# Two feed-forward layers' grouped residual updates moved from VectorE additions to ScalarE copies and accumulating transfers

## The chip, the cores and the metric

The kernel runs on one core of one Trainium2 chip. The metric is the device time of one execution in microseconds (us), the median of a few runs. One execution was also taken by the hardware profiler; its page and its trace are what is read here.

## The reference, cut to what matters

Two layers work on 512 latent tokens and 256 context tokens of width 1024. Each layer is an attention mixer followed by a SwiGLU feed-forward part, and each of the two adds its gated result to the residual stream. The parts that matter here:

```python
def swiglu(h, w_gate_up, w_down):
    g, u = jnp.split(h @ w_gate_up, 2, axis=-1)
    return (jax.nn.silu(g) * u) @ w_down
...
        h_lat = h_lat + g_a * o_lat
        h_lat = h_lat + g_f * swiglu(modulate(h_lat, sh_f, sc_f), ffn_w_gate_up[l], ffn_w_down[l])
        if ctx_out:
            h_ctx = h_ctx + cg_a * o_ctx
            h_ctx = h_ctx + cg_f * swiglu(modulate(h_ctx, csh_f, csc_f), ffn_w_gate_up[l], ffn_w_down[l])
    return rms_norm(h_lat, final_norm)
```

The inner width of the feed-forward part is 2816, that is 22 tiles of 128. `g_f` is one number per feature and stream (latent or context). Context tokens leave the computation after layer 0's feed-forward part, so layer 1 works on the 512 latent tokens alone there.

## The kernel before, in words

Activations are kept transposed: features on the 128 partitions, tokens along the row, so that a residual stream is eight tiles (m = 0 to 7) of 128 features by 768 tokens, of which layer 1 uses 512. Every matrix product is made of three products in a rounded format: each operand is split into a high part (a ScalarE copy that rounds) and a low part (the difference, on VectorE), and TensorE adds high x high, high x low and low x high (lines 319, 321 and 322 in `mm3`; lines 1414 to 1416 in `product`).

The feed-forward part (`ffn`, line 1514) walks through the 22 inner tiles in six groups (`CHUNKS`). For each inner tile, `Pair` loads a gate panel and an up panel (512 KB each, tiles `wr`, three buffers), makes weight combinations and splits on VectorE and ScalarE (`weights`, line 1426), and runs the products. After a group's inner tiles, the *down stage* follows: for each m, `load_w` (line 301) loads the group's part of the down weights (256 KB where the group has four inner tiles, 192 KB where it has three), ScalarE makes the high part (line 308, tiles `wh`, three buffers), VectorE the low part (line 309, tiles `wl`), and TensorE forms the group's contribution to feature tile m in PSUM banks. In layer 0 these are two banks per m (512 latent and 256 context tokens), in layer 1 one bank of 512. For all groups but the last, that contribution goes to the residual's home at once:

- Layer 0 (`down0`, line 1562): the residual lives in DRAM tiles `home`, one per m. GpSimd's queue issues a fetch of `home[m]` into an SBUF tile of the pool `p` (line 1255), VectorE computes bank times gate plus tile (line 1251, twice per m), and GpSimd's queue issues the write back (line 1568).
- Layer 1 (`down1`, line 1672): the residual lives in SBUF tiles `b` (the list `H`). VectorE adds bank times gate to it in place (line 1251, once per m). No transfer is made.

The last group of each layer goes through another function (`final0`, `final1`). `final0` fetches all eight `home` tiles into tiles `b` and adds to those; `final1` works on `H` in halves of 256 tokens and ends in the final norm. Both still use line 1251.

The pool `p` has eight buffers of 128 x 768, shared with two tiles per inner tile (`self.s`, `self.t`) and, in layer 0, with the scratch of `late_mods` (line 257), which computes layer 1's modulation on VectorE (line 273) from weights that GpSimd's queue fetches (line 263). Loads of weights are issued on SyncE's queue (line 134). The order of instructions on every engine is fixed when the program is built: a scheduler works through the code with a simulated timeline and puts each engine's instructions in a row, and every engine takes its row strictly in order, waiting on semaphores where a tile, a bank or a transfer is not ready. `behind` adds orderings for the scheduler.

Of the kernel before, what the change touches and what calls it, by code (L numbers as in the profile page):

```python
# [11 lines left out]
AF = mybir.ActivationFunctionType  # L12
ALU = mybir.AluOpType
# [6 lines left out]
NT = NL + NX  # L20
# [10 lines left out]
LATS = slice(0, NL)  # L31
# [67 lines left out]
def hybrid_kernel(ctx: ExitStack, tc, I, out):  # L99
# [6 lines left out]
    def T(tag, shape, dt=F32):  # L106
        count[0] += 1
        if tag not in SIZES:
            return sb.tile(shape, dt, tag=tag, name=f"{tag}_{count[0]}", bufs=BUFS.get(tag, 1))
        n = int(np.prod(shape[1:]))  # L110
        t = sb.tile([P, SIZES[tag] // (2 if dt == mybir.dt.bfloat16 else 4)], dt, tag=tag, name=f"{tag}_{count[0]}",
                    bufs=BUFS[tag])[: shape[0], :n]
        if len(shape) == 3:
            t = t.rearrange("p (a b) -> p a b", a=shape[1])
        return t

    def B(dt=F32, tag="b"):
        return T(tag, [P, NT], dt)

    def PS(tag):  # L120
        count[0] += 1
        return ps.tile([P, 512], F32, tag=tag, name=f"ps{tag}_{count[0]}", bufs=PBUFS[tag])
# [3 lines left out]
    def PG():  # L126

        ring[0] += 1
        return PS("stsdtsd"[ring[0] % 7])

    V, S, G, PE = nc.vector, nc.scalar, nc.gpsimd, nc.tensor
# [158 lines left out]
    def bg(n=1):  # L290

        for _ in range(n):
            next(mods, None)

    def mod(*which):
        while which not in MOD:
            bg()
        return MOD[which]
# [502 lines left out]
    fetched = []  # L801
# [6 lines left out]
    def chunk(comp, c):  # L808

        o, ins = PM(), []  # L810
        for k in range(KT):
            if k % 2 == 0:
                w = T("st", [P, 512]) if comp == 1 else T(("ph", "pl")[k // 2 % 2], [P, 512])
                fetch(w, I["mod_wp"][PE_MODS.index((0, comp)), c, k // 2])
            g = slice(32 * (k % 4), 32 * (k % 4) + 32)
            ins.append(PE.matmul(o[g, :NX], cond_col[:, k], w[:, NX * (k % 2) : NX * (k % 2) + NX], start=k < 4, stop=k > 3))
        run(ins[0], ins[-1])
        return o
# [54 lines left out]
    for k in range(KT):  # L873
        i = int(k > 5)
# [4 lines left out]
    scale = chunk(1, 0)  # L879
# [357 lines left out]
    H = []  # L1237
    for k in range(KT):
        t = B()
# [4 lines left out]
    def add_residual(m, o, l, comp, v, c, dst=None, base=None):  # L1244
        base = base or H[m]
        if c is TOK2:
            for x, v in pieces(c):
                ins = add_residual(m, o[:, x.start - HT : x.stop - HT], l, comp, v, x, dst, base)
            return ins
        g = mod(l, comp, v, m)  # L1250
        return V.scalar_tensor_tensor((dst or base)[:, c], o, g, base[:, c], op0=ALU.mult, op1=ALU.add)

    def fetched(m, c, tag="p"):
        t = B(tag=tag)
        G.dma_start(t[:, c], home[m][:, c])
        return t
# [61 lines left out]
    home = [dr.tile([P, NT], F32, name=f"home{k}") for k in range(KT)]  # L1318
# [241 lines left out]
    norm1, A = modulated(new, 1, 0, G, LATS)  # L1560

    def down0(m, w, hs):
        t = fetched(m, slice(0, NT))
        o = banks((LATS, CTXS), PG)
        mm3(o, w(), hs)
        for i, (x, c) in enumerate(o):
            ins = add_residual(m, x, 0, 5, i, c, None, t)
        G.dma_start(home[m], t)
        return ins

    def final0(src, hs):
# [5 lines left out]
    H = new  # L1577
# [3 lines left out]
    for k in range(KT):  # L1581
        t = dr.tile([P, NL], F32, name=f"parked{k}")
# [35 lines left out]
    for t0, n in ((0, 4), (4, 2)):  # L1618
        o = PS("t")
# [40 lines left out]
    H = []  # L1660
    for k in range(KT):
        t = B()
# [7 lines left out]
    fn = const("final_norm", [P, 8])  # L1670

    def down1(m, w, hs):
        o = PG()
        mm3([(o, LATS)], w(), hs)
        add_residual(m, o, 1, 5, 0, LATS)

    def final1(src, hs):

# [166 lines left out]
```

## Time and profile before

| what | value |
|---|---|
| times of three runs | 1554.84, 1552.52, 1556.6 us; median 1554.84 |
| profiled execution, first to last instruction (its span) | 1553.0 us, 1.84 us below the median of the three runs and inside their spread |
| busy: TensorE (PE), VectorE (DVE), ScalarE (ACT), GpSimd (POOL) | 98%, 76%, 49%, 13% of the span |
| mean granted TensorE clock | 0.996 |
| moved by transfers | 225.69 MB, mean 145 GB/s |
| feed-forward part of layer 0, of layer 1 | about 450 to 970 us, about 1180 to 1553 us |

How to read it: times inside the trace are microseconds from the span's start. A row of a group of instructions gives line, engine, operation, what it writes and reads, count, total busy time and mean duration in nanoseconds (ns), then the engine's idle time just before and what ended it. "PEld" is the load of weights into TensorE, which overlaps the products. Tiles are named by their pool (`p`, `b`, `wr`, `wh`, `wl`), PSUM banks by `pss`, `pst`, `psd`. Since a product's end is modelled, the time that TensorE loses is read from its waits rather than from its busy share.

### The profile page before, as it was taken

To read this page: it belongs to the slowest core of one execution; us is meant where nothing else is said; L and a number is where in the kernel's file an instruction comes from. 1 tells how busy PE (TensorE), PEld (TensorE's weight loads), DVE (VectorE), ACT (ScalarE), POOL (GpSimd) and SP (SyncE) were. 2 spreads that over 40 slices of the span, in tenths; PEclk is the share of its full clock that TensorE was granted. 3 is DMA by queue.
4 is the path that set the end of the run, shared out by engine and by line. 5 is a ranking of instruction groups with operands and counts; after the bars stand their busy time and mean duration, and the time that the engine had idled before them with its cause. 6 is when DMAs were issued, how large, how long until landed. Compare 5 with 4: busy or idle time off the path is not lost.

```text
span 1553.0 us, 26645 instructions
## 1 busy us (share of the span) xinstructions
PE 1527.4 (98%) x10048; PEld 1375.5 (89%) x10048; DVE 1179.9 (76%) x2418; ACT 758.2 (49%) x1521; POOL 195.1 (13%) x266
## 2 busy tenths in 40 slices
PE   9999999999999999999999999999999999999997
PEld 8788887878999898999989998877789899899997
DVE  4799877776867686777768667789977779678685
ACT  4532676674555242432424335567856445354453
POOL 0022211000111102012021122560011000000001
PEclk9999999999999999999999999999999999999999
DMA  9775654244643636547475493210214223324322
GB/s 320 251 226 176 165 129 106 57 131 136 217 138 119 232 104 216 173 133 287 128 261 175 156 355 137 59 37 1 96 58 161 70 84 127 115 75 136 89 91 87
DMA packets 80930, 225.69 MB, mean 145 GB/s; under 512 B 11232, under 2 KB 18400, under 8 KB 80800
## 3 DMA queue, kind: packets, MB, share of 16 engines
q1 hardware_dynamic: 61968, 148.47, 30.1%
q0 software_dynamic: 17680, 73.94, 13.9%
q8 instruction: 79, 1.29, 0.3%
q10 hardware_dynamic: 1152, 1.57, 0.3%
q14 instruction: 51, 0.42, 0.1%
HBM read 186.97 MB, written 23.07 MB: 135 GB/s over the span
## 4 chain that ended last, share of the span: by engine, by line
PE 85%; DVE 7%; DMA 3%; ACT 2%; issue 2%; POOL 0%; SPq 0%; DVEq 0%; ACTq 0%; POOLq 0%
PE pso L530 5%; PE pss L1416 5%; PE pss L1415 5%; PE pss L1414 5%; PE psd L319 4%; PE pss L319 4%; PE psd L321 4%; PE psd L322 4%; PE pss L322 4%; PE pss L321 4%; PE pst L1416 3%; PE pst L319 3%; PE pst L321 3%; PE pst L1414 3%; PE pst L322 3%; PE pst L1415 3%
## 5 line engine op out<-in xcount | busy, mean ns | idle before, releaser
L308 ACT CAST wh<-wr 128x1024 fp32r<-128x1024 f32 (+2 forms) x148 | 115.6, 795 | 225.1 <-DMA wr<-in_w_dn_dram 39.4
L309 DVE TENSOR_TENSOR wl<-wr,wh 128x1024 fp32r<-128x1024 f32 (+2 forms) x145 | 131.1, 911 | 82.3 <-ACT wh L308 78.1
L537 ACT ACTIVATE p<-p,sm 128x512 f32<-128x512 f32 (+3 forms) x144 | 105.0, 730 | 30.6 <-DVE sm L541 30.1
L1414 PE MATMUL pss<-b,wh 128*128 128x384 f32 (+1 forms) x346 | 107.6, 312 | 0.5 <-ACT b L345 0.5
L1415 PE MATMUL pss<-b,wh 128*128 128x384 f32 (+1 forms) x346 | 107.8, 312 | 0.0
L1416 PE MATMUL pss<-b,wl 128*128 128x384 f32 (+1 forms) x346 | 107.1, 311 | 0.0
L321 PE MATMUL psd<-b,wh 128*128 128x512 f32 (+2 forms) x254 | 88.7, 349 | 0.0
L273 DVE CUSTOM_DVE_ANT_0 p<-rope,cond 128x1024 bf16<-128x1024 f32 x64 | 76.9, 1221 | 12.4 <-DMA rope<-in_mod_w_dram 12.1
L319 PE MATMUL psd<-b,wh 128*128 128x512 f32 (+2 forms) x214 | 79.0, 369 | 0.7 <-ACT wh L308 0.3
L322 PE MATMUL psd<-b,wl 128*128 128x512 f32 (+2 forms) x214 | 77.8, 363 | 0.0
L263 POOL DMA_DIRECT2D rope<-in_mod_w_dram x48 | 25.6, 533 | 412.4 <-DVE mod L273 389.8
L530 PE MATMUL pso<-ph,b 128*64 128x256 f32 (+1 forms) x384 | 77.0, 359 | 0.2 <-DVE ph L475 0.2
L530 PE MATMUL pso<-pl,b 128*64 128x256 f32 (+1 forms) x384 | 76.9, 358 | 0.0
L1416 PE MATMUL pst<-b,wl 128*128 128x384 f32 (+1 forms) x226 | 70.8, 313 | 2.0 <-DVE wl L1402 2.0
L1414 PE MATMUL pst<-b,wh 128*128 128x384 f32 (+1 forms) x226 | 70.7, 313 | 0.6 <-ACT p L1464 0.6
L1401 ACT CAST wh<-pl 128x512 fp32r<-128x512 f32 x78 | 44.9, 619 | 53.0 <-PE pss L1415 22.7
L1415 PE MATMUL pst<-b,wh 128*128 128x384 f32 (+1 forms) x226 | 70.5, 312 | 0.0
L1401 ACT CAST wh<-wr 128x1024 fp32r<-128x1024 f32 x39 | 41.0, 1051 | 57.3 <-PE pst L1415 14.8
L321 PE MATMUL pss<-b,wh 128*128 128x256 f32 (+3 forms) x216 | 68.3, 316 | 0.0
L319 PE MATMUL pss<-st,wh 128*128 128x512 f32 (+2 forms) x198 | 67.5, 341 | 0.3 <-ACT wh L308 0.3
L322 PE MATMUL pss<-st,wl 128*128 128x512 f32 (+2 forms) x198 | 67.6, 341 | 0.1
L1414 PEld LDWEIGHTS pss<-b,wh 128*128 128x128 f32 x346 | 65.0, 188 | 1.0 <-ACT b L345 0.8
(609 smaller groups left out, 5269.4 us busy)
## 6 DMA issues: line engine op xcount, KB each, us to landing
wr<-in_w_gu_dram SPq DMA_DIRECT2D x88, 512.0 KB, 4.0
rope<-in_mod_w_dram POOLq DMA_DIRECT2D x48, 512.0 KB, 3.9
wr<-in_w_dn_dram SPq DMA_DIRECT2D x73, 256.0 KB, 3.0
wr<-in_w_out_dram SPq DMA_DIRECT2D x32, 512.0 KB, 3.8
p<-home POOLq DMA_DIRECT2D x40, 384.0 KB, 5.7
home<-p POOLq DMA_DIRECT2D x40, 384.0 KB, 5.6
wr<-in_w_in_dram SPq DMA_DIRECT2D x21, 512.0 KB, 3.9
ph<-in_mod_w_dram SPq DMA_DIRECT2D x24, 256.0 KB, 3.0
```

What stands on the lines that cost most here:

```text
L273: behind(V.tensor_tensor_reduce(out=T("p", [P, D], mybir.dt.bfloat16), in0=w, in1=cond[:, v, :], op0=ALU.mult, op1=ALU.add, scale=1.0, sca ...
L308: behind(S.copy(h, r), *after[:1])
L309: behind((G if eng else V).tensor_tensor(lo, r, f(h), op=ALU.subtract), *after[1:])
L319: ins = PE.matmul(o, wh[:, k], mh[:, c], start=first and k == 0, stop=False)
L321: PE.matmul(o, wh[:, k], ml[:, c], start=False, stop=False)
L322: PE.matmul(o, wl[:, k], mh[:, c], start=False, stop=last and k == n - 1)
L530: ins = PE.matmul(o[64 * i : 64 * i + 64, c], v(kt), t, start=n == 0, stop=n == len(moving[i]) - 1)
L537: S.activation(p[:, c], p[:, c], AF.Exp, bias=nm, scale=-1.0, accum_out=dn)
L1401: S.copy(h, t)
L1414: PE.matmul(o, wh, xh, start=first and k == 0, stop=False, skip_group_check=not first)
L1415: PE.matmul(o, wh, xl, start=False, stop=False, skip_group_check=not first)
L1416: PE.matmul(o, wl, xh, start=False, stop=k == 3, skip_group_check=not first)
```

## The change

Inside the groups, VectorE no longer makes the residual update. ScalarE copies the bank times the gate into a tile of the pool `p` (an ACTIVATE with Copy and a per-partition scale), and GpSimd's queue issues a transfer that adds this tile to the residual's home: in layer 0 to the DRAM tile `home[m]`, in layer 1 to the SBUF tile `H[m]`. Layer 0's fetch within groups disappears. The last group of each layer is as before.

```diff
+    def gated(dst, o, g):
+        return S.activation(dst, o, AF.Copy, scale=g)
+
...
     def down0(m, w, hs):
-        t = fetched(m, slice(0, NT))
+        t = B(tag="p")
         o = banks((LATS, CTXS), PG)
         mm3(o, w(), hs)
         for i, (x, c) in enumerate(o):
-            ins = add_residual(m, x, 0, 5, i, c, None, t)
-        G.dma_start(home[m], t)
+            ins = gated(t[:, c], x, mod(0, 5, i, m))
+        G.dma_start(home[m], t, accum_op=ALU.add)
         return ins
...
     def down1(m, w, hs):
-        o = PG()
+        o, t = PG(), B(tag="p")
         mm3([(o, LATS)], w(), hs)
-        add_residual(m, o, 1, 5, 0, LATS)
+        gated(t[:, LATS], o, mod(1, 5, 0, m))
+        G.dma_start(H[m][:, LATS], t[:, LATS], accum_op=ALU.add)
```

The new code is three lines longer above the feed-forward part, so the lines there are numbered higher by three (1401, 1402, 1436 become 1404, 1405, 1439); the copy is line 1254, the fetch of line 1255 becomes line 1258, the accumulating transfers are lines 1571 and 1679. The scheduler places the other instructions anew around it. TensorE has as many rows as before; where the order differs, a few products that used to stand early as fillers stand later.

On ScalarE, at the end of layer 1's first group, the high parts of the down weights (line 308) stood in one run before the next pair's weights (line 1401, tile `wr` to `wh`, `ph`):

```order
L308 CAST wh_13301<-wr_13299 128x384
L308 CAST wh_13318<-wr_13316 128x384
L308 CAST wh_13335<-wr_13333 128x384
L308 CAST wh_13352<-wr_13350 128x384
L308 CAST wh_13369<-wr_13367 128x384
L1401 CAST wh_13389<-wr_13385 128x1024
L1401 CAST ph_13413<-wr_13386 128x512
L1401 CAST wh_13391<-ph_13398 128x512
```

The same place now:

```order
L308 CAST wh_13325<-wr_13323 128x384
L1254 ACTIVATE p_13265<-pst_13264,mod_1831_8978 128x512
L308 CAST wh_13344<-wr_13342 128x384
L1254 ACTIVATE p_13284<-pss_13283,mod_1831_8978 128x512
L1404 CAST wh_13365<-wr_13361 128x1024
L1254 ACTIVATE p_13303<-psd_13302,mod_1831_8978 128x512
L1254 ACTIVATE p_13322<-pss_13321,mod_1831_8978 128x512
L1404 CAST ph_13389<-wr_13362 128x512
L1404 CAST wh_13367<-ph_13374 128x512
```

Each copy of a bank stands in ScalarE's row between the casts of weights, and the last ones stand among the casts of the next pair's weights.

On VectorE, at the same boundary, the preparation of the next pair (lines 1402 to 1444) stood among the last residual updates:

```order
L309 TENSOR_TENSOR wl_13370<-wr_13367,wh_13369 128x384
L1251 SCALAR_TENSOR_TENSOR b_12135<-psd_13332,mod_1831_9010,b_12135 128x512
L1402 TENSOR_TENSOR wl_13390<-wr_13385,wh_13389 128x1024
L1436 TENSOR_TENSOR pl_13397<-wr_13386 128x512
L1251 SCALAR_TENSOR_TENSOR b_12137<-pss_13349,mod_1831_9010,b_12137 128x512
L1437 TENSOR_TENSOR ph_13398<-pl_13397,wr_13385 128x512
L1440 TENSOR_TENSOR ph_13403<-wr_13385,wr_13386 128x512
L1251 SCALAR_TENSOR_TENSOR b_12139<-pst_13366,mod_1831_9010,b_12139 128x512
L1444 TENSOR_TENSOR pl_13409<-wr_13385,ph_13398 128x512
```

The same place now:

```order
L309 TENSOR_TENSOR wl_13345<-wr_13342,wh_13344 128x384
L1405 TENSOR_TENSOR wl_13366<-wr_13361,wh_13365 128x1024
L1439 TENSOR_TENSOR pl_13373<-wr_13362 128x512
L1440 TENSOR_TENSOR ph_13374<-pl_13373,wr_13361 128x512
L1443 TENSOR_TENSOR ph_13379<-wr_13361,wr_13362 128x512
L1447 TENSOR_TENSOR pl_13385<-wr_13361,ph_13374 128x512
```

The updates are gone from VectorE's row, and the preparation of the next pair follows the low parts directly.

On GpSimd's queue, at the end of layer 0's fifth group, writes back and fetches stood mixed; the fetches into `b` are those of `final0`:

```order
L1255 DMA b_9853<-home_4268 128x768
L1568 DMA home_4270<-p_9433 128x768
L1255 DMA p_9510<-home_4272 128x768
L1568 DMA home_4271<-p_9470 128x768
L1255 DMA b_9855<-home_4269 128x768
L1255 DMA b_9857<-home_4270 128x768
L1568 DMA home_4272<-p_9510 128x768
L1255 DMA b_9859<-home_4271 128x768
L1255 DMA b_9861<-home_4272 128x768
```

The same place now:

```order
L1571 DMA home_4271<-p_9432 128x768
L1258 DMA b_9807<-home_4265 128x768
L1258 DMA b_9809<-home_4266 128x768
L1258 DMA b_9811<-home_4267 128x768
L1258 DMA b_9813<-home_4268 128x768
L1571 DMA home_4272<-p_9471 128x768
L1258 DMA b_9815<-home_4269 128x768
L1258 DMA b_9817<-home_4270 128x768
L1258 DMA b_9819<-home_4271 128x768
L1258 DMA b_9821<-home_4272 128x768
```

The last accumulating transfer (into `home_4272`) is still followed by `final0`'s fetch of the same tile. In layer 1 the queue's row now holds forty accumulating transfers and nothing between them.

## The prediction

> **What bounds the kernel now.** I read the page's busy times first, then TensorE's waits in the two feed-forward stretches, then the busy times by stage. The page (busy us, share of the span, instructions):
>
> ```profile
> PE 1527.4 (98%) x10048; PEld 1375.5 (89%) x10048; DVE 1179.9 (76%) x2418; ACT 758.2 (49%) x1521; POOL 195.1 (13%) x266
> ```
>
> TensorE is the bound: it idles for 1553.0 - 1527.4 = 25.6 us in the whole span. VectorE, which the change relieves, is busy for 76%, so its work counts only where TensorE waits for it. The waits of TensorE between 480 and 935 us (layer 0's groups) and between 1230 and 1530 us (layer 1's), each with its sum, number and longest:
>
> ```profile
> PE pst L1416 <- DVE wl L1402: 2.0, 2, 1.4
> PE psd L319 <- DVE p L1251: 0.7, 1, 0.7
> ...
> PE pss L1416 <- DVE wl L1402: 0.6, 2, 0.3
> PE pst L319 <- ACT st L1401: 0.6, 1, 0.6
> ```
>
> These four rows are all there is: 2.7 us in layer 0 and 1.2 us in layer 1, 3.9 us or 0.25% of the time. No relief of an engine other than TensorE can bring more in these stretches. So the question is what of these 3.9 us goes, and what new waits the copies and transfers make.
>
> Busy times by stage: a down stage of layer 0 with the next pair's preparation, layer 1's first boundary, its third, and the pairs behind that. The columns are PE, PEld, DVE, ACT, POOL, the granted clock, the share of the transfer engines and GB/s:
>
> ```profile
> 595.00:640.00 45.00, 44.22 (x251) 39.58 (x250) 29.80 (x52) 11.36 (x19) 10.16 (x19) 1.00 0.72 252
> 1230.00:1250.00 20.00, 19.72 (x106) 16.53 (x105) 17.47 (x30) 8.20 (x16) 0.00 (x0) 1.00 0.46 136
> 1340.00:1358.00 18.00, 18.00 (x93) 15.10 (x92) 14.65 (x23) 7.27 (x13) 0.00 (x0) 1.00 0.55 164
> 1358.00:1402.00 44.00, 44.00 (x343) 42.54 (x343) 32.57 (x55) 22.45 (x45) 0.00 (x0) 1.00 0.24 78
> ```
>
> TensorE is full in all of them. VectorE is the second fullest at layer 1's boundaries (17.47 of 20 us), ScalarE has more than half its time free, and the transfer engines are already much in use in layer 0.
>
> **The change part by part.** *VectorE's updates go.* Their prices, by form:
>
> ```profile
> L1251 DVE SCALAR_TENSOR_TENSOR p<-psd,mod,p 128x512 f32<-128x512 f32 x15 | 11.2, 749 | 3.9 <-PE psd L322 3.5 <-DMA p<-home 0.4
> L1251 DVE SCALAR_TENSOR_TENSOR p<-pss,mod,p 128x256 f32<-128x256 f32 x15 | 7.2, 477 | 0.7 <-PE pss L322 0.7
> L1251 DVE SCALAR_TENSOR_TENSOR b<-pss,mod,b 128x512 f32<-128x512 f32 x19 | 14.2, 747 | 5.5 <-PE pss L322 5.5
> ```
>
> Layer 0 loses 40 x (0.749 + 0.477) = 49 us of VectorE, layer 1 40 x 0.747 = 30 us. All of it lies beside TensorE, except where a wait above hangs on it. Layer 0's longest of those, VectorE's rows and then TensorE's:
>
> ```profile
> 627.74 0.74 DVE L1251 SCALAR_TENSOR_TENSOR p<-pst,mod,p 128x512 f32<-128x512 f32 x1
> 629.60 0.48 DVE L1251 SCALAR_TENSOR_TENSOR p<-pss,mod,p 128x256 f32<-128x256 f32 x1
> 636.58 0.69 DVE L1436 TENSOR_TENSOR pl<-wr 128x512 f32<-128x512 f32 x1 [3.05 <-DMA wr<-in_w_gu_dram]
> ...
> 642.54 0.44 PE L1416 MATMUL pst<-b,wl 128*128 128x384 f32 x1 [1.35 <-DVE wl L1402]
> ```
>
> The two updates stand before the step that frees the buffer for the panel landing at 636.58. Without them the panel is asked for up to 0.74 + 0.48 = 1.2 us earlier; I credit 1.0 of this 1.4 us wait, and the same cause's other wait whole (2.0 - 1.4 = 0.6). The 0.7 us on line 1251 goes with the fetch it depended on. Layer 0 gains 2.3 us.
>
> *ScalarE's copies come.* No row before has a copy from a bank with a per-partition scale. The nearest rows are a copy from a bank with a fixed scale (lines 449 and 1095) and an ACTIVATE with a per-partition operand out of SBUF (line 407):
>
> ```profile
> L449 ACT ACTIVATE b<-psd 128x512 f32<-128x512 f32 x10 | 5.9, 590 | 8.7 <-PE psd L322 8.6
> L1095 ACT ACTIVATE b<-psd 128x256 fp32r<-128x256 f32 x8 | 3.0, 377 | 2.3 <-PE psd L322 2.3
> L407 ACT ACTIVATE b<-p,mod 128x512 fp32r<-128x512 f32 x16 | 11.6, 724 | 10.4 <-DVE mod L828 5.9 <-DVE p L406 4.5
> L407 ACT ACTIVATE b<-p,mod 128x256 fp32r<-128x256 f32 x16 | 7.9, 507 | 10.3 <-DVE p L406 10.3
> ```
>
> So 590 to 724 ns for 512 tokens, 377 to 507 for 256; I take 0.70 and 0.48, nearer to line 407, whose operands it has. Layer 0 adds 40 x 1.18 = 47 us, layer 1 40 x 0.70 = 28 us. At layer 1's third boundary ScalarE goes from 7.27 to 7.27 + 8 x 0.70 = 12.9 of 18 us: not full. The Trainium skill (ScalarE: Activation LUTs, Rules for kernel authors) speaks against the move: multiplications belong on VectorE, up to about three times faster there in bf16. The trace differs for this form, 590 to 724 ns against 747 for the update; by the rule, an estimate of 3 x 747 ns would make 8 copies last 17.9 us, and ScalarE would then be the bound of the down stages.
>
> A copy waits for its bank, and behind it in ScalarE's row stand casts of the next weights, for which VectorE's low parts and then TensorE wait. Before, the update stood in front of the low part in the same way, for 0.75 us; the copy puts 0.70 us in front of the cast instead. I count nothing, with bounds from -0.05 to +0.70 us at each of ten boundaries, most of it covered by ScalarE's idle time.
>
> *Layer 0's transfers.* The page's rows, with KB of one and median us to landing:
>
> ```profile
> p<-home POOLq DMA_DIRECT2D x40, 384.0 KB, 5.7
> home<-p POOLq DMA_DIRECT2D x40, 384.0 KB, 5.6
> ```
>
> Forty fetches go, and forty writes become accumulating ones. No row shows one. It costs at least one copy, and at most, by these rows, the fetch and the write it stands for, 5.7 + 5.6 = 11.3 us until landed. Layer 0's load on the transfer engines therefore falls or stays. The last one meets `final0`'s fetch; the rows of GpSimd's queue and of VectorE's last use:
>
> ```profile
> 923.95 0.54 POOL L1568 DMA_DIRECT2D home<-p  x1
> ...
> 930.46 0.54 POOL L1255 DMA_DIRECT2D b<-home  x1 [5.44 <-issue]
> ...
> 953.84 0.74 DVE L1251 SCALAR_TENSOR_TENSOR b<-pst,mod,b 128x512 f32<-128x512 f32 x1
> ```
>
> A landing of 11.3 us puts the fetch at about 935 us; with 5.7 us more its tile is there at 941, 13 us before its use. No cost.
>
> *Layer 1's transfers are new*: forty of 256 KB. GpSimd has nothing else to do there:
>
> ```profile
> POOL p L1711 <- ACT p L1707: 336.4, 1, 336.4
> ```
>
> But the transfer engines load weights there. A boundary adds 8 x 256 KB = 2.1 MB in 18 us, or 117 GB/s. By the first stage row (0.72 at 252 GB/s) that is a share of 0.33 at the price of one copy and 0.67 at two, on top of 0.55: 0.88 or 1.22. How long panel loads take in such a crowd is seen in layer 0 (612 to 632 us), and in layer 1 without it (1230 to 1300 us):
>
> ```profile
> L134 SPq DMA_DIRECT2D wr<-in_w_gu_dram x5: 327/328/1243, 614.6 to 631.3; - x5
> DMA to landing us min/median/max: 4.4/6.5/10.0
> ...
> L134 SPq DMA_DIRECT2D wr<-in_w_gu_dram x11: 327/328/328, 1236.9 to 1295.3; - x11
> DMA to landing us min/median/max: 3.5/4.1/4.6
> ```
>
> At one copy I expect layer 0's median: panels land 6.5 - 4.1 = 2.4 us later. What VectorE does between the second panel and TensorE's wait at the first boundary:
>
> ```profile
> 1243.28 0.69 DVE L1436 TENSOR_TENSOR pl<-wr 128x512 f32<-128x512 f32 x1
> 1243.88 0.75 DVE L1251 SCALAR_TENSOR_TENSOR b<-pss,mod,b 128x512 f32<-128x512 f32 x1
> ...
> 1245.74 0.74 DVE L1251 SCALAR_TENSOR_TENSOR b<-pst,mod,b 128x512 f32<-128x512 f32 x1
> ...
> 1247.60 0.69 DVE L1402 TENSOR_TENSOR wl<-ph,wh 128x512 fp32r<-128x512 f32 x1
> ...
> 1248.34 0.38 PE L1416 MATMUL pss<-st,wl 128*128 128x256 f32 x1 [0.28 <-DVE wl L1402]
> ```
>
> Two updates leave this chain, about 1.3 us (each is followed 0.66 us later by the next instruction). So 2.4 us late costs 1.1 us at this boundary and at the second, which waits as well (two waits in the row above). The other three show no wait, and I count none: their groups have four inner tiles, not three, so their loads are spread over a longer stage. Layer 1 loses 2.2 us.
>
> Sum: -2.3 + 2.2 = -0.1 us. On the profiled span that is 1552.9 us; on the median, which lies 1.84 us higher, **1554.7 us**.
>
> **The rivals.** *A, slower: the accumulating transfers crowd out layer 1's weight loads.* At two copies the share asked for is 1.22, more than there is, and panels land like layer 0's worst (10.0 us, 5.9 late), or midway (8.25 us, 4.15 late). At the first two boundaries lateness less 1.3 us becomes waiting; at the other three I count half of that. Midway: (4.15 - 1.3) x (2 + 1.5) = 10.0 us, less layer 0's 2.3: 1562.5 us. At the worst, 4.6 x 3.5 - 2.3 = +13.8: 1568.6 us. It decides, by more than 0.3%, from about 3.3 us of lateness (3.5 x 2.0 - 2.3 = 4.7). For it: layer 0's landings. Against it: the 44 us behind each boundary at a share of 0.24 can take what is late, and VectorE's relief of 8 x 0.66 us a boundary may buy more than 1.3. The Trainium skill (DMA: Bandwidth & Descriptors, Issuing engines are not separate DMA queues) states that transfers started from any queue run on the same 16 engines and interleave; by that, GpSimd's queue gives no protection, and layer 0's landings agree with it (4.4 to 10.0 us against 3.5 to 4.6).
>
> *B, slower: long landings hold the pool `p`.* The first update of layer 1's first group and the next pair's first write into `p`:
>
> ```profile
> 1233.44 0.75 DVE L1251 SCALAR_TENSOR_TENSOR b<-pst,mod,b 128x512 f32<-128x512 f32 x1 [0.49 <-PE pst L322]
> ...
> 1246.90 0.36 ACT L1454 COPY p<-pss 128x256 f32<-128x256 f32 x1
> ```
>
> Eight copies take all eight buffers, so that write now needs an early transfer landed within about 13.5 us. Beyond it, each us costs 1 us at five boundaries: a landing of 18.5 us gives +25, 1580 us. Above the 11.3 us bound; nothing in the trace asks for it.
>
> *C, faster: all 3.9 us go and nothing is added*: 1550.9 us. That is 0.25%; it needs run-to-run scatter as well to pass for faster.
>
> **How the numbers follow.** 0.3% is 4.7 us, about what a measurement of this kernel can tell from no change. The forecast (both sides' small waits, within 4.7 us) gets 0.60, A 0.26, B 0.07, and a result faster by more than 0.3% 0.07, C with scatter. So faster 0.07, same 0.60, slower 0.33. The range goes from C less half a us, 1550.4, to A's worst, 1568: below lie some 0.06, above some 0.10. The forecast's own range is 1550.4 to 1559.5.
>
> **What would show it.** Right: TensorE's waits still sum to a few us in both stretches, the wait on line 1251 is gone, the copy takes 0.6 to 0.72 us, panels in layer 1's boundaries land in 5 to 7.5 us, and the accumulating transfers in under 11.3 us. Panels at 4 us with waits gone speak for C; panels over 7.4 us with waits of TensorE on line 1402's low parts or ScalarE's casts on panels for A; line 1457's copies waiting for an accumulating transfer for B. The prediction is wrong if the change lands outside 1550.4 to 1568 us, or if its waits come from another place, such as ScalarE's casts behind a copy.

## The result, and the profile after

The changed kernel takes 1594.05 us (median of 4 runs, 1592.39 to 1599.06), the kernel before 1555.72 us beside it (4 runs). The ratio is 1.0259, with a 95% interval of 1.0242 to 1.0275: 38 us slower, far outside the range that was forecast. The profiled execution has a span of 1590.5 us, 37.5 us more than before.

The page's busy times (busy us, share of the span, instructions):

```profile
PE 1541.7 (97%) x10048; PEld 1385.0 (87%) x10048; DVE 1113.1 (70%) x2298; ACT 818.3 (51%) x1641; POOL 222.0 (14%) x266
```

VectorE's busy time fell by 67 us and ScalarE's rose by 60 us (the prediction had 79 and 75, adding up durations that overlap in the trace), and the time did not fall with it: TensorE now idles for 1590.5 - 1541.7 = 48.8 us, where it idled for 25.6. It is also busy for 14.3 us longer with the same number of products; part of that is its clock (last section). TensorE's waits in the changed kernel, in layer 0 (480 to 960 us) and in layer 1 (1240 to 1545 us), each with sum, number and longest, the smallest rows left out:

```profile
PE pss L1417 <- ACT p L1457: 9.5, 5, 5.2
PE pst L1419 <- DVE wl L1405: 1.1, 1, 1.1
PE pst L1417 <- ACT p L1467: 0.6, 1, 0.6
...
```

```profile
PE pss L1417 <- ACT wh L1404: 7.3, 6, 1.5
PE pst L1417 <- ACT wh L1404: 2.8, 2, 1.5
PE pss L1419 <- DVE wl L1405: 1.9, 5, 0.5
PE psd L1417 <- ACT wh L1404: 1.6, 1, 1.6
PE pst L1419 <- DVE wl L1405: 1.0, 1, 1.0
...
```

In place of the 2.7 and 1.2 us of before stand 12 us in layer 0 and 16 us in layer 1 (the smallest rows included). Most are waits for ScalarE's casts (line 1404) and copies of banks (1457) and for VectorE's low parts (1405), of the pairs that follow a boundary between groups. Both engines are late and not busy. This is the stage around layer 1's third boundary in the changed kernel, with the columns of the prediction's stages:

```profile
1362.00:1388.00 26.00, 22.78 (x125) 19.74 (x124) 14.84 (x23) 13.18 (x24) 6.12 (x8) 0.95 0.94 238
```

Over the five boundaries VectorE is busy for 54 to 57% of such a stage and ScalarE for 46 to 56%. What is full are the transfer engines, at a share of 0.78 to 0.94, where it was 0.45 to 0.52 before. What VectorE and ScalarE are late for is seen in the landings of the panels, in layer 1 (before, then after):

```profile
L134 SPq DMA_DIRECT2D wr<-in_w_gu_dram x38: 327/328/328, 1236.9 to 1493.4; - x38
...
DMA to landing us min/median/max: 3.4/3.7/5.7
```

```profile
L134 SPq DMA_DIRECT2D wr<-in_w_gu_dram x38: 327/328/881, 1249.5 to 1532.0; - x38
...
  DVE pl L1439: 21.4, 9
  ACT ph L1404: 12.8, 8
  ACT wh L1404: 12.5, 5
...
DMA to landing us min/median/max: 3.4/6.0/8.8
```

The same 38 loads land 2.3 us later at the median, and VectorE and ScalarE now wait 47 us for them, where they waited for 8. In layer 0 the median went from 5.3 to 7.4 us. The new transfers are the reason to look at first (the page's issues, KB of one, median us to landing):

```profile
home<-p POOLq DMA_DIRECT2D x40, 384.0 KB, 8.4
...
b<-p POOLq DMA_DIRECT2D x40, 256.0 KB, 6.7
```

To tell the two layers apart I measure two stretches in each trace, because what lies ahead of them varies by some us from one profile to the next. Layer 0 is from the first product of its first pair to the first transfer that parks the residual: 485.4 us before, 498.5 after, **+13.1 us**. Layer 1 is from the first product of its first pair to the start of TensorE's last instruction: 301.4 us before, 325.0 after, **+23.6 us**. The stretch between them is 0.5 us shorter, what precedes them 1.2 us longer: together the 37.4 us of the span. (The first two inner tiles of layer 0 and the first three of layer 1 are made outside `Pair`. The first pair meant here is the first that `Pair` makes, so that layer 1's stretch begins inside its first boundary.) In four of the kernels below layer 0 is left as before, and its stretch came out 1.0 to 1.5 us shorter there; so nothing under 2 us is read from one stretch.

Followed product by product (the starts of the rows of line 1414, now 1417, in their order), the delay grows at the boundaries alone: by about 2.8, 3.3, 5.6, 6.5 and 5.6 us at the five of layer 1, and by 1.2, -0.9, 3.6, 2.2 and 7.0 us at the five of layer 0.

### The profile page after: what moved, and what is told of

It is laid out like the page before. It is cut to its first block, busy times and chain, and to the rows that moved or that the text cites. A ratio compares the mean times of both kernels' runs of the same rounds, so it can differ in the third digit from the quotient of the medians.

```text
span 1590.5 us, 26703 instructions
## 1 busy us (share of the span) xinstructions
PE 1541.7 (97%) x10048; PEld 1385.0 (87%) x10048; DVE 1113.1 (70%) x2298; ACT 818.3 (51%) x1641; POOL 222.0 (14%) x266
## 4 chain that ended last, share of the span: by engine, by line
PE 76%; DMA 9%; DVE 8%; ACT 4%; issue 3%; POOL 0%; DVEq 0%; ACTq 0%; POOLq 0%
DMA wr<-in_w_gu_dram 8%; PE pso L530 5%; PE pss L1419 4%; PE pss L1417 4%; PE pss L1418 4%; PE psd L319 3%; PE pss L319 3%; PE psd L321 3%; PE psd L322 3%; PE pss L321 3%; PE pss L322 3%; PE pst L1419 3%; PE pst L1417 3%; PE pst L1418 3%; PE pst L484 3%
## 5 line engine op out<-in xcount | busy, mean ns | idle before, releaser
L1417 PE MATMUL pss<-b,wh 128*128 128x384 f32 (+1 forms) x346 | 109.7, 317 | 3.8 <-ACT wh L1404 3.3
L1418 PE MATMUL pss<-b,wh 128*128 128x384 f32 (+1 forms) x346 | 109.4, 316 | 0.1
L1679 POOL DMA_DIRECT2D b<-p x40 | 34.6, 878 | 274.5 <-ACT p L1254 222.3
L1439 DVE TENSOR_TENSOR pl<-wr 128x512 f32<-128x512 f32 x39 | 26.9, 689 | 62.6 <-DMA wr<-in_w_gu_dram 62.6
L1419 PEld LDWEIGHTS pss<-b,wl 128*128 128x128 f32 x346 | 66.4, 192 | 3.2 <-DVE wl L1405 3.1
```

Source lines behind the costliest of these rows:

```text
L1417: PE.matmul(o, wh, xh, start=first and k == 0, stop=False, skip_group_check=not first)
L1418: PE.matmul(o, wh, xl, start=False, stop=False, skip_group_check=not first)
L1419: PE.matmul(o, wl, xh, start=False, stop=k == 3, skip_group_check=not first)
```

## The experiments

Three causes were held against each other. *Transfers*: the accumulating transfers fill the transfer engines where the panels of the next pairs are loaded, as rival A said. *ScalarE's time*: the copies hold back the casts. *Turned rows*: without VectorE's updates the scheduler wrote the preparation of the pairs in another order. This is the second pair behind the third boundary of layer 1, VectorE's row before and after (1402 and 1405 with a row of 1024 make the gate panel's low part; the other lines combine gate and up panel):

```
before                                   after
L1436 pl<-wr            (up)             L1439 pl<-wr            (up)
L1455 p<-pss,p                           L1440 ph<-pl,wr
L1402 wl<-wr,wh 1024    (gate, low)      L1443 ph<-wr,wr
L1437 ph<-pl,wr                          L1458 p<-pss,p
L1440 ph<-wr,wr                          L1447 pl<-wr,ph
L1444 pl<-wr,ph                          L1405 pl<-wr,ph         (up, low)
L1402 pl<-wr,ph         (up, low)        L1405 wl<-wr,wh 1024    (gate, low)
```

The gate panel's low part has gone from third place to last, behind everything that needs the up panel, which lands later. On ScalarE the up panel's cast (line 1404, `ph`) now stands ahead of the gate panel's (`wh`). The casts are turned so in three of layer 1's 19 pairs, the second behind the third, the fourth and the fifth boundary. The result is a wait of TensorE for a cast whose panel had long landed. The changed kernel there, two rows of ScalarE and then one of TensorE:

```profile
1380.25 0.62 ACT L1404 CAST ph<-wr 128x512 fp32r<-128x512 f32 x1 [2.71 <-DMA wr<-in_w_gu_dram]
1380.77 1.04 ACT L1404 CAST wh<-wr 128x1024 fp32r<-128x1024 f32 x1
...
1381.86 0.39 PE L1417 MATMUL pss<-b,wh 128*128 128x256 f32 x1 [1.38 <-ACT wh L1404]
```

ScalarE stood idle for 2.71 us until the up panel landed, cast that, and only then cast the gate panel, for which TensorE stood.

The results in one table: median us, ratio to the kernel before with its 95% interval, and the two stretches against before.

| kernel | us | ratio | layer 0 | layer 1 |
|---|---|---|---|---|
| the change | 1594.05 | 1.0259 [1.0242, 1.0275] | +13.1 | +23.6 |
| tiny | 1561.04 | 1.0039 [1.0024, 1.0055] | -3.9 | +10.0 |
| plain | 1565.86 | 1.0076 [1.0044, 1.0109] | -3.3 | +16.4 |
| xfer | 1575.90 | 1.0130 [1.0097, 1.0163] | -1.4 | +19.0 |
| gfirst | 1599.24 | 1.0272 [1.0236, 1.0307] | +11.9 | +21.9 |
| rtiny | 1560.82 | 1.0030 [1.0016, 1.0044] | -3.8 | +7.9 |
| rafter | 1593.95 | 1.0249 [1.0217, 1.0282] | +13.2 | +21.8 |
| rpool | 1581.86 | 1.0168 [1.0146, 1.0189] | -1.0 | +28.1 |
| late | 1579.33 | 1.0153 [1.0134, 1.0172] | -1.5 | +23.4 |
| rtiny2 | 1552.95 | 0.9976 [0.9958, 0.9995] | -4.0 | +1.6 |
| rafter2 | 1588.13 | 1.0182 [1.0146, 1.0219] | +15.7 | +13.7 |
| late2 | 1555.70 | 0.9992 [0.9970, 1.0014] | -1.4 | +0.4 |
| rall | 1572.50 | 1.0101 [1.0078, 1.0125] | +12.9 | +2.5 |
| twice | 1576.74 | 1.0144 [1.0124, 1.0164] | +10.1 | +9.5 |

### tiny: the copies without the transfers

```diff
-        G.dma_start(home[m], t, accum_op=ALU.add)
+        G.dma_start(home[m][:, :8], t[:, :8], accum_op=ALU.add)
-        G.dma_start(H[m][:, LATS], t[:, LATS], accum_op=ALU.add)
+        G.dma_start(H[m][:, :8], t[:, :8], accum_op=ALU.add)
```

> Copies as in the change, but each accumulating transfer moves only 8 of its 768 or 512 columns, in both layers; the rest of the addition is left out. The scheduler then puts the up panel's cast ahead of the gate panel's on ScalarE in six of layer 1's pairs, where the change has it in three and the kernel before in none. Theory T (transfers: the accumulating transfers fill the transfer engines, the next panels land late, TensorE waits): 1549 to 1557 us, panels in layer 1 land in about 3.7 us again. Rival R (ScalarE's row: the copies and the turned order of the casts hold back the high parts): 1580 to 1605 us, with TensorE's waits on ScalarE's casts of layer 1 at 11.7 us or more.

1561.04 us: between the two theories. Layer 0 is 3.9 us shorter than before, so there all of the loss, and more, hangs on the transfers. Layer 1 still loses 10.0 us, although its panels land in 4.2 us at the median. Its waits (1225 to 1510 us) are for low parts on VectorE, the engine that was relieved:

```profile
PE pss L1419 <- DVE wl L1405: 4.3, 5, 1.8
PE psd L1419 <- DVE wl L1405: 1.9, 1, 1.9
```

### plain: the same bytes, the same rows, no addition

```diff
-        G.dma_start(home[m], t, accum_op=ALU.add)
+        G.dma_start(home[m], t)
-        G.dma_start(H[m][:, LATS], t[:, LATS], accum_op=ALU.add)
+        G.dma_start(H[m][:, LATS], t[:, LATS])
```

> The change with plain writes in place of the accumulating transfers, so the old residual is overwritten instead of added to; same bytes, same order of every engine row for row. T, with the price of an accumulating transfer at about two copies: one copy is left, layer 1 loses 8 to 14 us instead of 24 and layer 0 0 to 5 instead of 12, in all 1563 to 1574 us. T, if only the bytes count: 1590 to 1596 us. R: the rows are the same, so 1588 to 1596 us.

1565.86 us, in the range for an accumulating transfer that costs two copies, but by luck: layer 1 lost more than the 8 to 14 us expected, 16.4, and layer 0 gained 3.3 us where none was expected. The price is seen directly in the transfer engines' time (queue, packets, MB, share of the 16 engines), layer 1 after (1240 to 1530 us) and with plain writes (1225 to 1505 us):

```profile
q0 software_dynamic: 5760, 10.49, 21.2%
```

```profile
q0 software_dynamic: 3200, 10.49, 9.3%
```

For the same 40 transfers that is 0.212 x 290 = 61.5 us against 0.093 x 280 = 26.0 us of all engines, or 1.54 against 0.65 us for one: 2.4 copies, in 144 packets in place of 80. With the rows unchanged, 7.2 us of layer 1's loss (23.6 - 16.4) come with the addition. The other 16.4 us split only roughly, into 10.0 us for rows (from tiny, whose rows are not quite the change's) and 6.4 us for plain bytes. Layer 0 gains 3.3 us with plain writes, so its 13.1 us come with the accumulating form; rall and twice ask why.

### xfer: the transfers without the copies

```diff
         add_residual(m, o, 1, 5, 0, LATS)
+        G.dma_start(spare[m], H[m][:, LATS], accum_op=ALU.add)
```

(`spare` stands for eight regions in two tiles that are no longer read.)

> The kernel before, with VectorE's updates in both layers, and in layer 1 one more accumulating transfer of 256 KB per feature tile, from the updated residual to tiles that nobody reads. The gate panel's cast stays ahead of the up panel's in all of layer 1. T: layer 1 loses 15 to 30 us, 1570 to 1585 us in all. R: 1554 to 1558 us, since ScalarE's row is that of before.

1575.90 us, layer 1 +19.0, with VectorE's updates and the gate panel first. Its panels landed in 5.6 us at the median (at most 8.6). So the transfers are enough by themselves: about 2.5 to 5.1 us at each of the five boundaries.

### gfirst, rtiny, rafter: part of the old order

```diff
-            parts(g, *w1, self.after)
+            gate = S.copy(w1[0], g)
+            low = behind(V.tensor_tensor(w1[1], g, f(w1[0]), op=ALU.subtract), *self.after)
...
-            V.tensor_tensor(s4, g[:, h[1]], s2, op=ALU.subtract)
+            behind(V.tensor_tensor(s4, g[:, h[1]], s2, op=ALU.subtract), *(low,) * self.l)
-            self.u2 = parts(u[:, h[1]], T("ph", [P, 512], F32R), T("pl", [P, 512], F32R))
+            up = T("ph", [P, 512], F32R), T("pl", [P, 512], F32R)
+            behind(S.copy(up[0], u[:, h[1]]), *(gate,) * self.l)
+            marks["low"] = V.tensor_tensor(up[1], u[:, h[1]], f(up[0]), op=ALU.subtract)
+            self.u2 = up
```

gfirst has only the ordering of the two casts, on the change; rtiny has both orderings on tiny, rafter both on the change.

> The change with one more ordering, in layer 1 only: the up panel's cast stands behind the gate panel's of the same pair, as it does before. T: the three waits of 1.6 us behind it go in part, 1582 to 1592 us. R: layer 1's loss of 24 us shrinks to under 12, 1570 to 1582 us.

> As the run with 8 columns per transfer (1558.5 us in its profile, of which layer 1's feed-forward part lost 10.0 us against the kernel before), and in layer 1 two orderings more: the gate panel's cast stands ahead of the up panel's on ScalarE, and the gate panel's low part ahead of the last combination (pl from ph) on VectorE. If the turned rows made the 10 us (theory R2): layer 1 loses under 3 us, 1549 to 1553 us in all, since layer 0 gained 3.9. If it is ScalarE's time for the copies (R1): layer 1 still loses 8 us or more, 1556 to 1562 us.

> The change with the same two orderings in layer 1, its full transfers kept. T (transfers) with R2 added to it: layer 1 loses 14 to 19 us instead of 23.6, 1583 to 1590 us in all. T alone, the rows only showing what the late panels leave: 22 us or more, 1590 us or more. R2 alone: under 5 us, 1572 to 1577 us.

gfirst, at 1599.24 us, missed both of its ranges; the scheduler had then put the gate panel's low part behind the last combination in 7 of the 19 pairs in place of 4. The 1.7 us that it won in layer 1 are less than a stretch can tell, and its profile is of an execution 8.4 us below its median. rtiny won 2.1 of 10.0 us and rafter 1.8, which is, within 0.2 us, what was expected if the turned rows cost nothing. By these numbers ScalarE's time for the copies was left. But the rows of rtiny said otherwise: the low part stood fourth of five, ahead of the last combination as asked, where before it stood second. The edit had not restored what it was to test.

### rtiny2, rafter2: the old order, pair by pair

```diff
+            at = 0 if not self.l else 1 if self.j < 9 else 2 if self.j % 2 else 4
+            behind(V.tensor_tensor(s1, u[:, h[0]], u[:, h[1]], op=ALU.add), *self.after, *(low,) * (at == 1))
+            behind(V.tensor_tensor(s2, s1, g[:, h[0]], op=ALU.subtract), *(low,) * (at == 2))
+            behind(V.tensor_tensor(s4, g[:, h[1]], s2, op=ALU.subtract), *(low,) * (at == 4))
```

(These lines replace those that make `s1`, `s2` and `s4`; the cast's ordering is kept.)

> As the run with 8 columns per transfer, and in layer 1 the preparation of each pair is put back into the order that VectorE and ScalarE have in the kernel before: the gate panel's cast ahead of the up panel's, and the gate panel's low part ahead of the first, second or fourth combination, as it stands there pair by pair. The first two orderings alone had left 7.9 of 10.0 us of layer 1's loss. R2 (the turned rows): layer 1 loses under 3 us, 1549 to 1553 us in all. R1 (ScalarE's time for the copies): still 6 us or more, 1555 to 1562 us.

> The change, full transfers, with the same order of the kernel before in layer 1's pairs. If transfers and rows each cost their own: layer 1 loses 12 to 17 us in place of 23.6, 1581 to 1588 us in all. If late panels are enough by themselves, as in the run with transfers alone (19.0 us): 18 to 24 us, 1588 to 1595 us.

With the low part where it stood before in each pair, layer 1 of rtiny2 loses 1.6 us instead of 10.0, and the whole takes 1552.95 us. Its waits in the stretch (1230 to 1510 us) are the few of before:

```profile
PE pst L319 <- ACT st L1404: 0.6, 1, 0.6
PE psd L1419 <- DVE wl L1437: 0.5, 1, 0.5
PE pss L1417 <- ACT p L1462: 0.3, 1, 0.3
```

So the turned rows are shown, and ScalarE's time for the copies costs nothing that can be read. rafter2 takes the same order with the full transfers: +13.7 instead of +23.6. The rows are worth 8.4 us without the transfers and 9.9 with them, so the two causes add up. What rafter2 wins lies at the third to fifth boundaries (4.1, 3.6 and 2.3 us), where the casts had been turned. Its layer 0, which the edit leaves alone, came out at +15.7, and its profile is of the fastest of four executions: the median, 1588.13 us, lies 5.9 us under the change's and between the two expected ranges.

### rpool: GpSimd adds, without a transfer

```diff
-        G.dma_start(H[m][:, LATS], t[:, LATS], accum_op=ALU.add)
+        G.tensor_tensor(H[m][:, LATS], H[m][:, LATS], t[:, LATS], op=ALU.add)
```

Layer 0 is that of before, the two orderings of rtiny are kept.

> Layer 0 as before; in layer 1 ScalarE copies bank times gate as in the change, and GpSimd adds the copy to the residual in SBUF, with no transfer; the two orderings are kept. T: no transfer, so 1553 to 1557 us, panels in layer 1 land in about 3.7 us. R1: ScalarE's copies are there, 1560 to 1566 us. A third way, not seen in any run so far: GpSimd's additions slow VectorE's instructions beside them; then VectorE's mean for the low parts rises above its 0.69 us and the time goes over 1560 us.

1581.86 us, and by the third way. The groups of the low parts of the down weights, before (1235 to 1520 us) and here, and then GpSimd's additions:

```profile
L309 DVE TENSOR_TENSOR wl<-wr,wh 128x512 fp32r<-128x512 f32 x25 | 16.9, 687 | 19.5 <-ACT wh L308 19.5
```

```profile
L309 DVE TENSOR_TENSOR wl<-wr,wh 128x512 fp32r<-128x512 f32 x24 | 26.0, 1104 | 19.6 <-ACT wh L308 17.1 <-PE pst L322 1.2 <-PE pss L322 1.2
```

```profile
L1683 POOL TENSOR_TENSOR b<-b,p 128x512 f32<-128x512 f32 x40 | 66.0, 1668 | 248.2 <-ACT p L1254 205.2 <-DVE wl L309 42.9
```

VectorE's subtraction of two SBUF tiles takes 1104 ns in place of 687 beside GpSimd's addition of 1668 ns. (In rtiny, with the same copies and the same rows but no addition on GpSimd, it takes 692.) The Trainium skill (SBUF — State Buffer, Who interferes with whom) states that a VectorE instruction with two SBUF inputs contends with a GpSimd instruction that reads SBUF; the trace agrees, with 417 ns on the mean.

### late, late2: the same transfers at another time

```diff
-        o, t = PG(), B(tag="p")
+        o, t = PG(), slots[m]
-        G.dma_start(H[m][:, LATS], t[:, LATS], accum_op=ALU.add)
+        waiting.append((H[m][:, LATS], t))
...
                     hs.append(p.dst)
+                    if l and waiting and j == k0 + 1:
+                        held = G.tensor_copy(zeros, p.s[:, :1])
+                        while waiting:
+                            behind(G.dma_start(*waiting.pop(0), accum_op=ALU.add), held)
```

The copies go to eight tiles of their own, and a group's transfers start when the second pair of the next group has its first activation. Layer 0 is that of before. late lacks the `behind` of the last line and has the orderings of rtiny, late2 those of rtiny2.

> Layer 0 as before; in layer 1 the copies go to eight tiles of their own, and the accumulating transfers of a group are held until the second pair of the next group has begun, where the transfer engines were little used (a share of 0.24 in the kernel before); the two orderings are kept. T, with the place deciding: layer 1 loses 0 to 4 us, 1553 to 1560 us. T, with the bytes deciding wherever they are: 1565 to 1575 us. R1: 1560 to 1566 us with TensorE's waits at the boundaries, not behind them.

> As the run that was to hold back layer 1's accumulating transfers, where the scheduler had put them ahead of the instruction that holds them; now each stands behind it on GpSimd's queue, and the pairs have the order of the kernel before. Layer 0 as before. T, the place deciding: layer 1 loses 0 to 4 us, 1554 to 1560 us. T, the bytes deciding wherever they are: 1565 to 1575 us.

late, at 1579.33 us outside all its ranges, told nothing on the place: nothing tied the transfers to the small copy, and the scheduler put them ahead of it, so they started in the down stages as in the change. In late2 they stand behind it, on GpSimd's row:

```profile
1303.52 0.40 POOL L1547 COPY zeros<-p 128x1 f32<-128x1 f32 x1 [39.61 <-ACT p L1464]
1303.97 3.53 POOL L1549 DMA_DIRECT2D b<-cond  x4
1306.12 3.15 POOL L1549 DMA_DIRECT2D b<-rope  x2
1307.20 3.85 POOL L1549 DMA_DIRECT2D b<-nb  x2
```

and TensorE waits in layer 1 (1225 to 1510 us) in one place only:

```profile
PE pst L319 <- ACT st L1404: 0.6, 1, 0.6
```

1555.70 us, no difference from before. The same forty accumulating transfers, eight in a bunch, cost 0.4 us here against 13.7 us in the down stages with the same row order (rafter2). In four of the five groups behind them one panel still landed 6.8 to 8.3 us after its issue, but behind the boundary, and TensorE did not wait for it. The tiles of their own, the other difference from rafter2, had nothing to relieve: in rafter2 no instruction waited for the landing of a copy's transfer. That late2 is not faster than before, with 30 us less work on VectorE, shows what the relief is worth where TensorE waited for 1.2 us.

### rall, twice: layer 0

Layer 0's 13.1 us stayed to be explained, since fetch and write together cost what one accumulating transfer does. GpSimd's queue in layer 0, before (480 to 950 us) and after (480 to 960 us):

```profile
q0 software_dynamic: 13466, 57.95, 35.0%
```

```profile
q0 software_dynamic: 12962, 42.66, 35.3%
```

That is 164.5 us of all engines before and 169.4 after. rall is late2 with the change's `down0`, and with the pair behind each boundary of layer 0 in its old order:

```diff
-            at = 0 if not self.l else 1 if self.j < 9 else 2 if self.j % 2 else 4
+            at = {4: 2, 8: 1, 12: 4, 16: 4, 20: 4}.get(self.j, 0) if not self.l else 1 if self.j < 9 else 2 if self.j % 2 else 4
```

> The whole change, with layer 1's transfers held as in the run where that worked (layer 1 lost 0.4 us there), and in layer 0 the first pair behind each boundary put back into the order of the kernel before: gate panel's cast ahead of the up panel's, gate panel's low part where it stood. Layer 0's accumulating transfers stay where the change has them. If layer 0's 13.1 us come from the turned rows: layer 0 loses under 4 us, 1553 to 1560 us in all. If they come from the transfers that now fall into the down stages: 9 us or more, 1565 to 1572 us.

+12.9 us and 1572.50 in all: the rows are not layer 0's cause. In rall as in the change, more than half of layer 0's loss arises at the last boundary. The changed kernel there, ScalarE's rows and then TensorE's longest wait:

```profile
923.59 0.62 ACT L1404 CAST ph<-wr 128x512 fp32r<-128x512 f32 x1 [4.62 <-DMA wr<-in_w_gu_dram]
927.01 0.83 ACT L1404 CAST nb<-wr 128x768 fp32r<-128x768 f32 x1 [2.81 <-DMA wr<-in_w_dn_dram]
...
929.73 0.47 ACT L1457 COPY p<-pss 128x384 f32<-128x384 f32 x1
...
930.26 0.69 PE L1417 MATMUL pss<-st,wh 128*128 128x384 f32 x1 [5.19 <-ACT p L1457]
```

The copy of a bank, for which TensorE waits, stands behind two casts that wait for a late panel and for a late load of down weights.

twice is plain with each write issued a second time, to a place that nobody reads:

```diff
         G.dma_start(home[m], t)
+        G.dma_start(again[m], t)
...
         G.dma_start(H[m][:, LATS], t[:, LATS])
+        G.dma_start(spare[m], t[:, LATS])
```

> The run with plain writes, and behind each of them a second plain write of the same tile to a place that nobody reads, in both layers: two copies' engine time in the down stages, in plain form, with no fetch ahead of them. Layer 0 lost 13.1 us with accumulating transfers and gained 3.3 with one plain write. If the engine time that falls into the down stages decides: layer 0 loses 8 to 15 us. If the accumulating form decides, at the same engine time: layer 0 stays between a gain of 4 and a loss of 3 us. Layer 1, by the engine time: 8 to 15 us lost, as in the run with accumulating transfers in the old row order (13.7); by the form: under 6.

Layer 0 loses 10.1 us and layer 1 9.5, in plain form. So a loss of this size needs no addition: a second copy is enough (its queue moved 57.74 MB in layer 0 at 33.5%, nearly as in the kernel before). The scheduler wrote twice's rows in an order nearer to the old one, so its layer 1 is to be held against rafter2's 13.7 and not against 23.6. And the loss lies elsewhere: behind the last boundary of layer 0 twice is 2.8 us late and the change 13.2, and twice loses the rest in the last pairs and the last group. It does not show, then, that the change loses its 13.1 us in the same way. What may have spared the kernel before is where its fetches lie. GpSimd's queue around the third boundary of layer 0, before:

```profile
688.48 0.54 POOL L1255 DMA_DIRECT2D p<-home  x1
694.86 0.53 POOL L263 DMA_DIRECT2D rope<-in_mod_w_dram  x1 [5.84 <-DVE mod L273]
695.38 1.07 POOL L1255 DMA_DIRECT2D p<-home  x2
704.56 0.53 POOL L263 DMA_DIRECT2D rope<-in_mod_w_dram  x1 [8.10 <-DVE mod L273]
705.32 0.54 POOL L1568 DMA_DIRECT2D home<-p  x1 [0.22 <-issue]
```

Three of the eight fetches have gone out 10 to 17 us ahead of the first write; after, nothing can start before the copy. That this is the difference was not tried by itself, and the traces bear it out only in part. From a boundary's first write to 12 us after its last, GpSimd's queue takes more engine time than before at all five (4.2, 7.6, 2.1, 2.8 and 2.1 us of all engines), but the loss does not follow these amounts: it is largest at the fifth, and at the second 0.9 us is won. That the accumulating transfers make layer 0's loss is shown (tiny, plain, rall); why they cost more than a fetch and a write of the same total is open.

## Why the prediction was wrong, point by point

In short: layer 0's transfers, put at no cost, made 13.1 us where a gain of 2.3 stood in the sum. In layer 1 late panels cost 13.7 us where 2.2 stood, and turned rows, which had no term, 8.4 to 9.9.

**What bounds the kernel.** Right: TensorE, and nothing but its waits in these stretches counted. rtiny2, with hardly any transfer, shows the most that was to be had: 0.24%, which is rival C's 0.25%.

**VectorE's updates go.** Layer 0's -2.3 us is of the right size or small: tiny, rtiny and rtiny2 have -3.8 to -4.0 us there, against -1.0 to -1.5 in the kernels that leave layer 0 as before. The relief in layer 1 was put at 1.3 us where it counted; rafter2 against xfer (13.7 against 19.0) has 5.3 us over five, about 1.1 on the mean, though most of it lies at the third boundary.

**ScalarE's copies.** The prices were right, 0.70 and 0.48 us forecast; 256 tokens took 466 to 475 ns on the mean, and of 512 this is the form in layer 1, of 13:

```profile
L1254 ACT ACTIVATE p<-pst,mod 128x512 f32<-128x512 f32 x13 | 8.9, 684 | 0.0
```

"I count nothing" was right for the copies' time (rtiny2, +1.6 us). Here is the first step that failed, one that the prediction does not have: taking the updates out of VectorE's row changed what the scheduler put where they had stood. Only the first boundary's rows were read, where the gate panel still came first. In the second pair behind the third, fourth and fifth, its cast had gone behind the up panel's and its low part to the end: 8.4 to 9.9 us.

**Layer 0's transfers.** "Layer 0's load on the transfer engines therefore falls or stays" was nearly right in its amount (164.5 and 169.4 us), and the landing of 8.4 us at the median kept the bound of 11.3 us, though the longest took 14.1. The step that failed is the one from this to "No cost": the cost was +13.1 us (tiny, rall), on ScalarE's row, where bank copies stand behind casts of late loads. The amount was priced over the layer, while the panels are loaded in the down stages. At the last boundary the prediction asked only whether `final0`'s tile comes in time, and it did; but 7.0 us are lost there, since the panels of the next pairs, loaded in the same crowd, land after 5.8 to 11.5 us in place of 3.5 to 7.7.

**Layer 1's transfers.** "At one copy I expect layer 0's median", 2.4 us later: the lateness was right (3.7 to 6.0 us), but by luck, since the price was 2.4 copies and not one. What failed is the step from lateness to cost. It took 1.1 us at two boundaries and none at the other three, because those showed no wait before and their loads were thought to be spread. With the old row order (rafter2) the five cost about 2.5, 3.8, 1.5, 2.9 and 3.3 us, 13.7 us in the stretch where the sum had 2.2: a stage without a wait before is not a stage with slack. One reason can be read from the queue, though no run tried it alone. With three buffers, the fourth panel is asked for when VectorE is through with the first: at each boundary 12 to 13 us after the first was, 10 us before, so a late panel makes a later one late. In the changed kernel TensorE's clock added to it at three of the five boundaries (below).

**The rivals.** A named one of the two causes and its price, and was too small by far: 8 to 14 us forecast as its loss, 38 measured. It halved three boundaries that were hit like the others and had no term for the rows, and none for layer 0. Its own sign, panels over 7.4 us, did not come at the median: lateness of 2.3 us was enough, where A counted on 3.3 us or more. B did not come: no copy of line 1457 waited for a landing. Its waits on ScalarE (9.5 us in layer 0) look alike, but ScalarE stood on casts of late panels ahead of it in its row.

**The numbers.** The range ended at 1568.0. Its upper end was A's worst case; the two other costs were in no case.

## What to carry to other kernels

In this case an accumulating transfer took the engine time of two copies or a little more. It is to be priced at the stage where it is issued: the share of the transfer engines over a layer says nothing about the stage in which the next weights are loaded. Where a scheduler writes the rows, an instruction that is taken out moves its neighbours, and the rows of every boundary have to be compared, not only those of the first. To move work from a full row, start its transfers where a late load makes nobody wait (late2), and expect no gain where the engine that bounds did not wait.

## What the runs showed of the hardware

At the third to fifth boundary of layer 1, TensorE came back from waits at half its clock, though none of them was long. The changed kernel around the third boundary of layer 1 and at the fourth and fifth (the columns are those of the stages above: PE, PEld, DVE, ACT, POOL, granted clock, share of the transfer engines, GB/s):

```profile
1381.00:1385.00 4.00, 1.30 (x7) 0.89 (x7) 4.00 (x7) 2.52 (x5) 0.00 (x0) 1.00 0.53 97
1385.30:1388.60 3.30, 3.30 (x18) 3.30 (x17) 0.79 (x2) 0.37 (x1) 0.00 (x0) 0.50 0.80 299
1388.60:1392.00 3.40, 3.40 (x30) 3.40 (x30) 1.40 (x4) 1.64 (x4) 0.00 (x0) 0.99 0.01 5
...
1454.00:1457.50 3.50, 3.50 (x20) 3.50 (x20) 0.42 (x1) 0.37 (x1) 0.00 (x0) 0.58 0.73 268
1521.00:1525.00 4.00, 4.00 (x24) 4.00 (x23) 0.69 (x2) 0.37 (x1) 0.00 (x0) 0.60 0.62 231
```

In 3.3 us 18 products start, in the next 3.4 us 30: about 1.2 us is lost after the wait, at a granted clock of 0.50. The waits ahead of it were of 1.4 and 1.5 us, 2.2 us apart, and one of 0.4 us behind them. Idle time as such does not do it: xfer idles for 17.5 us in layer 1, with waits of up to 1.9 us, and its clock does not fall there. The Trainium skill (TensorE: Matmul & The Clock Gate, HAM oscillation — how this bites in real kernels) states that a wait for a transfer which lasts past an idle window brings half the clock back, and this case agrees in kind; here two shorter waits were enough, with TensorE busy for 1.3 of the 4 us in which they lie.

GpSimd needs longer to issue an accumulating transfer. Its issues of the write before and of the accumulating transfer after (ns, least, median and most):

```profile
L1568 POOL DMA_DIRECT2D home<-p x40: 539/544/547, 516.5 to 923.9; - x40
```

```profile
L1571 POOL DMA_DIRECT2D home<-p x40: 856/870/908, 518.0 to 930.1; - x40
```
